# One block sum of the linear-attention branch by a DMA that adds within SBUF, and two weight splits written ahead of other steps

## The chip, the cores and the metric

The kernel runs on one core of a Trainium2 chip. The metric is the device time of one execution in microseconds. Three runs of the kernel before gave 763.68, 763.93 and 764.01 us; their median is 763.93 us.

## The reference

One layer of a decoder on 512 tokens with 16 meta tokens in front, width 1024: two branches, retention and gated linear attention (GLA), both fed by one input projection, each projected back to the width and merged by learned gates.

```
u = rms_norm(h, norm_gain)
proj = u @ w_in
(rq, rk, rv, rg, gq, gk, gv, gg, glr, m_ret, m_gla) = jnp.split(proj, points, axis=-1)
...
o_gla = gla_chunked(gq, gk, gv, log_a)
o_gla = head_rms_norm(o_gla, gla_norm_gain...).reshape(bsz, length, GLA_WIDTH)
o_gla = o_gla * jax.nn.silu(gg)

merged = sigmoid(m_ret) * (o_ret @ w_branch_ret) + sigmoid(m_gla) * (o_gla @ w_branch_gla)
return h + merged @ w_out
```

The change lies in `o_gla @ w_branch_gla`, a product of 512 x 1024 by 1024 x 1024 in float32. All else is as before.

## The kernel before, in words

**Products.** Float32 operands are split into a high part (a cast, on ScalarE, ACT in the profile) and a low part (operand minus high part, on VectorE, DVE), both in the type fp32r (line 154, `split`). Each block product is then three matmuls on TensorE (PE): high by high, high of the weights by low of the input, low of the weights by high of the input (line 318). PE is fed the whole time by such products, 24 matmuls each of 128x128 by 128x256 where a 512 x 512 block is multiplied.

**Seven products for eight.** `quad` multiplies a 2 x 2 arrangement of blocks by Winograd's scheme with seven products, numbered 1 to 7. The input's seven forms are made once: A11, A12, A22 (blocks) and S1 to S4 (sums of blocks). The weights' forms are made in each call: w11, w21 and w22 are loaded by DMAs from SP's queue, x3 and x1 are loaded the same way and then added to by a second DMA from GpSimd's queue (POOL, line 282, `accum_op`), and w11 += x3 (for product 6) and w21 += w11 (for product 4) are additions on DVE. Three PSUM tiles b, a and c take the products. `copy` moves a tile from PSUM to SBUF on ACT (line 334), `evac` adds two of them into an output block.

**GLA's branch.** `gla_branch` calls `quad` twice (j = 0 and 1, names `bg0` and `bg1` in the order of the program, both `bg` in the profile) with `early=True`: products in the order 1, 7, 6, 2, 5, 4, 3. The output blocks, `gb`, go to a buffer `kept` in DRAM by DMAs from SP's queue. The next call is the first `quad` of retention's query and key, `rqk`.

**The forms** are made in `gla_sums`, which runs beside the products, a step between two of them. There a00, a01, a10 and a11 are the blocks of GLA's output, 128 x 1024 each (tiles `og`, `og1gq`, `og`, `og1gk`). DVE turns a10 into the sum for S1 and a00 into the sum for S2. For S4 GpSimd adds a00 to a01 (line 1115), and ACT and DVE split the negative of the result (lines 1125 and 1126). The tiles of the forms' parts are `ga` (A11, A12), `ga22h` and `ga22l` (A22), `gs` (S1, S2, S4) and `gs3h`, `gs3l` (S3).

**What sets the order.** Each engine works its own queue strictly in order, and the order in a queue follows from the order of the code and from a scheduling layer that places instructions by their dependencies; a few are pinned by hand with `after`. PE's order is fixed: `pin` ties each product to the one before. Three tiles each for high and low weight parts go round (`wsplit`), so a split waits for the product three back in that ring. Six tiles `raw` hold loaded weights: SP's next load starts when DVE has read the last of an old tile. Loads and stores from SP, and the adding DMAs from POOL, share 16 DMA engines; in the profile q1 is SP's queue, q0 is POOL's.

## Time and profile before

| | |
|---|---|
| median of 3 runs | 763.93 us (763.68 to 764.01) |
| profiled execution, first to last instruction (span) | 762.2 us |
| median less span: what lies around the span | 1.7 us |
| PE busy | 750.4 us, 98% of the span |
| DVE busy | 611.2 us, 80% |
| ACT busy | 451.2 us, 59% |
| POOL busy | 133.4 us, 17% |
| mean granted TensorE clock | 0.996 of full speed |

No time is given for the profiled execution apart from its span. In the timeline's rows the first number is the start and the second the busy time in us, then engine, line, operation, out<-in, shapes; in brackets the engine's idle time ahead of the row and what ended it. Several equal rows that follow each other are one row with a count. Numbers of tiles are left out, so `bg_l<-bg_w,bg_h` is the low part of any of a call's weights, told apart by the order.

### The profile page before, as it was taken

The numbers are of one execution on the slowest core, as the hardware profiler recorded it, in microseconds if no ns is written. First come the engines' busy times: TensorE is split into PE (matmuls) and PEld (weight loads), VectorE is DVE, ScalarE is ACT, GpSimd is POOL, SyncE is SP. The second block draws the span as 40 slices with busy tenths as digits, with TensorE's granted clock in tenths as the row PEclk, the third lists the DMA queues.
The fourth block names the chain that finished last, engine by engine and source line by source line (L and its number), as shares of the span: only waits on it lengthen the run. The fifth ranks groups of instructions, "written<-read, shape, count | busy, mean of one in ns | idle before, by whom it ended". The sixth has DMA issues, their size and how long they took to land.

```text
span 762.2 us, 14057 instructions
## 1 busy us (share of the span) xinstructions
PE 750.4 (98%) x5595; PEld 701.5 (92%) x5595; DVE 611.2 (80%) x873; ACT 451.2 (59%) x764; POOL 133.4 (17%) x172
## 2 busy tenths in 40 slices
PE   9999999999989999999999999999999999999996
PEld 6799899999989999998889999889999999988996
DVE  6799877689897799778957688876787989775994
ACT  7897584666974465545646455555554756532562
POOL 2211200112231122110330100240002210111142
PEclk9999999999999999999999999999999999999999
DMA  9864321822568973753684563696477357687503
GB/s 301 277 146 106 89 84 45 185 82 70 137 168 229 295 171 91 164 144 119 176 239 125 117 161 111 166 206 154 120 166 159 93 148 193 227 196 199 136 29 111
DMA packets 99995, 116.89 MB, mean 153 GB/s; under 512 B 5717, under 2 KB 90837, under 8 KB 99673
## 3 DMA queue, kind: packets, MB, share of 16 engines
q1 hardware_dynamic: 79896, 88.19, 37.8%
q0 software_dynamic: 19744, 27.27, 19.6%
q8 instruction: 44, 0.72, 0.4%
q10 hardware_dynamic: 288, 0.53, 0.2%
q14 instruction: 23, 0.18, 0.1%
HBM read 104.44 MB, written 11.53 MB: 152 GB/s over the span
## 4 chain that ended last, share of the span: by engine, by line
PE 87%; DVE 9%; issue 2%; ACT 1%; POOL 0%; POOLq 0%; DVEq 0%
PE rv_b L318 6%; PE rg_b L318 6%; PE rqk_b L318 5%; PE rqk_c L318 4%; PE br_p L192 4%; PE br_p L193 3%; PE br_p L189 3%; PE gg_b L318 3%; PE mr_b L318 3%; PE gv_p L640 3%; PE rv_c L318 3%; PE bg_b L318 3%; PE rg_c L318 3%; PE mg_b L318 2%; PE gg_c L318 2%
## 5 line engine op out<-in xcount | busy, mean ns | idle before, releaser
L192 PE MATMUL br_p<-ol,br_h 128*128 128x512 f32 x128 | 50.6, 395 | 1.7 <-DVE ol L492 1.7
L189 PE MATMUL br_p<-oh,br_h 128*128 128x512 f32 x128 | 50.4, 394 | 0.0
L193 PE MATMUL br_p<-oh,br_l 128*128 128x512 f32 x128 | 50.3, 393 | 0.0
L154 ACT CAST rv_h<-rv_w 128x1024 fp32r<-128x1024 f32 x24 | 25.2, 1052 | 26.9 <-DVE rv_w L371 9.6
L154 DVE TENSOR_TENSOR rv_l<-rv_w,rv_h 128x1024 fp32r<-128x1024 f32 x24 | 29.3, 1221 | 9.2 <-ACT rv_h L154 9.2
L154 DVE TENSOR_TENSOR rg_l<-rg_w,rg_h 128x1024 fp32r<-128x1024 f32 x20 | 24.4, 1219 | 8.4 <-ACT rg_h L154 8.4
L192 PEld LDWEIGHTS br_p<-ol,br_h 128*128 128x128 f32 x128 | 24.0, 188 | 7.4 <-DVE ol L492 2.4
L154 ACT CAST br_h<-br_w 128x1024 fp32r<-128x1024 f32 x16 | 16.8, 1050 | 23.4 <-PE br_p L192 9.9
L282 POOL DMA_DIRECT2D rqk_x<-in_w_in_dram x8 | 10.4, 1305 | 109.5 <-DVE vl L154 66.2
L193 PEld LDWEIGHTS br_p<-oh,br_l 128*128 128x128 f32 x128 | 24.0, 188 | 5.5
L154 ACT CAST rg_h<-rg_w 128x1024 fp32r<-128x1024 f32 x20 | 21.0, 1052 | 13.2 <-PE br_p L192 5.0
L189 PEld LDWEIGHTS br_p<-oh,br_h 128*128 128x128 f32 x128 | 24.0, 188 | 5.1 <-ACT oh L491 0.2
L318 PE MATMUL rv_b<-rv_l,fh 128*128 128x256 f32 x96 | 27.1, 282 | 0.1
L318 PE MATMUL rqk_b<-fh,rqk_h 128*128 128x256 f32 (+1 forms) x96 | 27.2, 283 | 0.0
L318 PE MATMUL rqk_b<-fh,rqk_l 128*128 128x256 f32 (+1 forms) x96 | 27.1, 282 | 0.0
L318 PE MATMUL rqk_b<-fl,rqk_h 128*128 128x256 f32 (+1 forms) x96 | 27.1, 282 | 0.0
L154 DVE TENSOR_TENSOR rqk_l<-rqk_w,rqk_h 128x1024 fp32r<-128x1024 f32 x20 | 24.4, 1220 | 3.3 <-ACT rqk_h L154 3.3
L318 PE MATMUL rg_b<-rg_h,fl 128*128 128x256 f32 x96 | 27.0, 281 | 0.0
L318 PE MATMUL rv_b<-rv_h,fl 128*128 128x256 f32 x96 | 27.0, 281 | 0.0
L318 PE MATMUL rg_b<-rg_h,fh 128*128 128x256 f32 x96 | 26.9, 281 | 0.0
L318 PE MATMUL rg_b<-rg_l,fh 128*128 128x256 f32 x96 | 26.9, 281 | 0.0
L318 PE MATMUL rv_b<-rv_h,fh 128*128 128x256 f32 x96 | 26.9, 280 | 0.0
(720 smaller groups left out, 3239.4 us busy)
## 6 DMA issues: line engine op xcount, KB each, us to landing
rv_w<-in_w_in_dram SPq DMA_DIRECT2D x16, 512.0 KB, 4.2
br_w<-in_w_branch_ret_dram SPq DMA_DIRECT2D x16, 512.0 KB, 3.5
rqk_w<-in_w_in_dram SPq DMA_DIRECT2D x12, 512.0 KB, 4.5
rg_w<-in_w_in_dram SPq DMA_DIRECT2D x12, 512.0 KB, 5.4
rqk_x<-in_w_in_dram SPq DMA_DIRECT2D x8, 512.0 KB, 5.3
rqk_x<-in_w_in_dram POOLq DMA_DIRECT2D x8, 512.0 KB, 8.1
rg_x<-in_w_in_dram SPq DMA_DIRECT2D x8, 512.0 KB, 4.2
rg_x<-in_w_in_dram POOLq DMA_DIRECT2D x8, 512.0 KB, 7.7
```

The lines of the kernel that those rows point to most:

```text
L154: return nc.scalar.copy(hi, src), nc.vector.tensor_sub(lo, src, hi.bitcast(F32))
L189: m = nc.tensor.matmul(o, lh, rh, start=first, stop=False)
L192: nc.tensor.matmul(o, lh, rl, start=False, stop=False)
L193: m = nc.tensor.matmul(o, ll, rh, start=False, stop=last)
L282: x = nc.gpsimd.dma_start(t, block(0, 1), accum_op=ALU.add)
L318: m = nc.tensor.matmul(ps[t][:, :n] if wide else ps[t], l, r, start=first and j == 0, stop=kk == 3 and j == 2, skip_group_check=not fresh ...
L640: m = nc.tensor.matmul(pss[t], (al if j == 1 else ah)[t // 2, kh][:, k, c], (lo if j == 2 else hi)[:, kk, :], start=q == kk == j == 0, sto ...
```

## The change

Two edits. In `gla_sums` GpSimd's addition of a00 into a01 becomes a DMA from GpSimd's queue that adds a01 into a00, both in SBUF, 512 KB; S4's two parts are then split from a00, and `after` places them behind the last weight split written before them (`low`). In `quad`, for calls with `early`, the split of x1 for product 5 is written right behind product 2, ahead of the addition w21 += w11, of the output block `put(0, 0)` and of the copy of tile c; the addition moves behind the next step; the split of w22 for product 3 is written ahead of `put(0, 1)`. Other calls pass `ready=None` and make the splits where they did. PE's order of instructions is the same, row for row.

```diff
@@ quad, early
             product(2, A12, w21, a, True)
-            nc.vector.tensor_add(w21, w21, w11)
+            ready = prepare(5, x1)
             put(0, 0, a, x)
             x7 = copy(c, 3)
             yield
+            nc.vector.tensor_add(w21, w21, w11)
...
-        product(5, S1, x1, b, False)
+        product(5, S1, x1, b, False, ready)
...
         product(4, A22, w21, c, False)
+        ready = prepare(3, w22) if early else None
         put(0, 1, c, y)
         yield
-        product(3, S4, w22, b, False)
+        product(3, S4, w22, b, False, ready)
@@ gla_sums
-        nc.gpsimd.tensor_add(a01, a01, a00)
+        nc.gpsimd.dma_start(a00, a01, accum_op=ALU.add)
...
-        nc.scalar.mul(hi, a01, -1.0)
-        nc.vector.scalar_tensor_tensor(lo, a01, -1.0, hi.bitcast(F32), op0=ALU.mult, op1=ALU.subtract)
+        after(nc.scalar.mul(hi, a00, -1.0), low[0])
+        after(nc.vector.scalar_tensor_tensor(lo, a00, -1.0, hi.bitcast(F32), op0=ALU.mult, op1=ALU.subtract), low[1])
```

DVE's queue in the first branch call (`bg0`), from the low part for product 2 to the first split of the second call, before; `gs1`, `gs4` are the low parts of S1 and S4, `gb0` and `gb1` output blocks:

```order
L154 TENSOR_TENSOR bg0_2_l_2761<-bg0_w21_2654,bg0_2_h_2760 128x1024
L154 TENSOR_TENSOR gs1_2504<-og0_1331,gs1_2504 128x1024
L365 TENSOR_TENSOR bg0_w21_2654<-bg0_w21_2654,bg0_w11_2653 128x1024
L154 TENSOR_TENSOR bg0_5_l_2797<-bg0_x1_2656,bg0_5_h_2796 128x1024
L154 TENSOR_TENSOR ga22l0_2512<-og1gk_2521,ga22h0_2510 128x512
L154 TENSOR_TENSOR bg0_4_l_2832<-bg0_w21_2654,bg0_4_h_2831 128x1024
L1164 TENSOR_TENSOR gb0_2789<-bg0_a_2666,bg0_x1_2696 128x512
L154 TENSOR_TENSOR ga22l1_2513<-og1gk_2521,ga22h1_2511 128x512
L1126 SCALAR_TENSOR_TENSOR gs4_2503<-og1gq_2520,gs4_2503 128x1024
L1162 SCALAR_TENSOR_TENSOR gb1_2824<-bg0_b_2665,bg0_x3_2792 128x512
L154 TENSOR_TENSOR bg0_3_l_2865<-bg0_w22_2657,bg0_3_h_2864 128x1024
L154 TENSOR_TENSOR bg1_1_l_2911<-bg1_w11_2895,bg1_1_h_2910 128x1024
```

The same stretch of DVE's queue now:

```order
L154 TENSOR_TENSOR bg0_2_l_2761<-bg0_w21_2654,bg0_2_h_2760 128x1024
L154 TENSOR_TENSOR bg0_5_l_2789<-bg0_x1_2656,bg0_5_h_2788 128x1024
L154 TENSOR_TENSOR gs1_2504<-og0_1331,gs1_2504 128x1024
L369 TENSOR_TENSOR bg0_w21_2654<-bg0_w21_2654,bg0_w11_2653 128x1024
L154 TENSOR_TENSOR ga22l0_2512<-og1gk_2521,ga22h0_2510 128x512
L154 TENSOR_TENSOR ga22l1_2513<-og1gk_2521,ga22h1_2511 128x512
L1167 TENSOR_TENSOR gb0_2792<-bg0_a_2666,bg0_x1_2696 128x512
L154 TENSOR_TENSOR bg0_4_l_2832<-bg0_w21_2654,bg0_4_h_2831 128x1024
L154 TENSOR_TENSOR bg0_3_l_2860<-bg0_w22_2657,bg0_3_h_2859 128x1024
L1165 SCALAR_TENSOR_TENSOR gb1_2824<-bg0_b_2665,bg0_x3_2795 128x512
L1129 SCALAR_TENSOR_TENSOR gs4_2503<-og0_1331,gs4_2503 128x1024
L154 TENSOR_TENSOR bg1_1_l_2911<-bg1_w11_2895,bg1_1_h_2910 128x1024
```

The split for product 5 moved two places up, that for product 4 two places down, that for product 3 ahead of `gb1` and S4's, and S4's low part down to the place ahead of the second call's first split.

ACT's queue over the same stretch, before; the copies are of PSUM tiles:

```order
L154 CAST bg0_2_h_2760<-bg0_w21_2654 128x1024
L154 CAST gs1_2504<-og0_1331 128x1024
L154 CAST bg0_5_h_2796<-bg0_x1_2656 128x1024
L154 CAST ga22h0_2510<-og1gk_2521 128x512
L1125 ACTIVATE gs4_2503<-og1gq_2520 128x1024
L334 COPY bg0_x2_2758<-bg0_b_2665 128x512
L154 CAST bg0_4_h_2831<-bg0_w21_2654 128x1024
L154 CAST ga22h1_2511<-og1gk_2521 128x512
L154 CAST bg0_3_h_2864<-bg0_w22_2657 128x1024
L334 COPY bg0_x3_2792<-bg0_c_2667 128x512
```

And now:

```order
L154 CAST bg0_2_h_2760<-bg0_w21_2654 128x1024
L154 CAST bg0_5_h_2788<-bg0_x1_2656 128x1024
L154 CAST gs1_2504<-og0_1331 128x1024
L154 CAST ga22h0_2510<-og1gk_2521 128x512
L334 COPY bg0_x2_2758<-bg0_b_2665 128x512
L154 CAST ga22h1_2511<-og1gk_2521 128x512
L154 CAST bg0_4_h_2831<-bg0_w21_2654 128x1024
L154 CAST bg0_3_h_2859<-bg0_w22_2657 128x1024
L334 COPY bg0_x3_2795<-bg0_c_2667 128x512
L1128 ACTIVATE gs4_2503<-og0_1331 128x1024
```

S4's high part moved from ahead of the copy of tile b to behind the copy of tile c. In the second branch call and in all other calls the order on ACT and DVE stays. SP's queue, before:

```order
L280 DMA bg1_w21_2896<-in_w_branch_gla_dram 128x4x256
L280 DMA bg1_x1_2898<-in_w_branch_gla_dram 128x4x256
L280 DMA bg1_w22_2899<-in_w_branch_gla_dram 128x4x256
L1166 DMA kept_116<-gb0_2789 128x2x256
L1166 DMA kept_116<-gb1_2824 128x2x256
L280 DMA rqk0_w11_3139<-in_w_in_dram 128x4x256
```

and now, with the loads of the second branch call (`bg1`), stores of output blocks and the first load of `rqk`:

```order
L280 DMA bg1_w21_2896<-in_w_branch_gla_dram 128x4x256
L280 DMA bg1_x1_2898<-in_w_branch_gla_dram 128x4x256
L1169 DMA kept_116<-gb0_2792 128x2x256
L280 DMA bg1_w22_2899<-in_w_branch_gla_dram 128x4x256
L280 DMA rqk0_w11_3139<-in_w_in_dram 128x4x256
L1169 DMA kept_116<-gb1_2824 128x2x256
```

A store moved ahead of a load and the next call's first load ahead of a store. The raw tiles that the first two loads go to changed places: the load of w21 now waits for DVE's split of x1 (product 5's), that of x1 for the addition w21 += w11; before it was the other way round. On POOL the addition's place is taken by the DMA; it stands behind the adding DMA of the second call's x3 and ahead of that of its x1, waits for DVE's low part of S2, and no longer for the low part of A12, since it doesn't write to a01.

## The prediction

> **What bounds the kernel now.** I read the page's first part, then PE's waits over the whole kernel, then PE's timeline at the largest of them. The first part:

> ```profile
> PE 750.4 (98%) x5595; PEld 701.5 (92%) x5595; DVE 611.2 (80%) x873; ACT 451.2 (59%) x764; POOL 133.4 (17%) x172
> ```

> PE is busy nearly throughout: only a wait of PE, or a stretch in which its clock is lower, is there to be won. PE's waits, as instruction, releaser, and total, count and longest in us:

> ```profile
> PE br_p L192 <- DVE ol L492: 1.7, 2, 0.9
> PE bg_b L318 <- DVE bg_l L154: 1.3, 1, 1.3
> PE bg_b L318 <- ACT bg_x L334: 0.8, 1, 0.8
> ```

> The second and third lie in the branch. PE's timeline there:

> ```profile
> 222.72 0.28 PE L318 MATMUL bg_a<-ga,bg_l 128*128 128x256 f32 x1
> 223.77 0.50 PE L318 MATMUL bg_b<-gs,bg_h 128*128 128x256 f32 x2 [0.77 <-ACT bg_x L334]
> 225.56 0.38 PE L318 MATMUL bg_b<-gs,bg_l 128*128 128x256 f32 x1 [1.29 <-DVE bg_l L154]
> 229.77 0.28 PE L318 MATMUL bg_c<-ga22h,bg_h 128*128 128x256 f32 x1
> 232.60 0.40 PE L318 MATMUL bg_b<-gs,bg_h 128*128 128x256 f32 x2
> ```

> The rows are the end of product 2, the start of product 5, its first matmul with the weights' low part, and the starts of products 4 and 3, in `bg0`. PE waits first for the copy that frees tile b, then for the low part of x1: 0.77 + 1.29 = 2.06 us. The chain of waits gives what stood ahead of that low part on DVE, and how long 22 and 24 matmuls took on PE:

> ```profile
> 223.16 1.21 DVE bg_w L365
> 224.37 1.15 DVE bg_l L154
> 225.56 4.37 PE bg_b L318 x22
> ...
> 241.28 2.74 PE bg_b L318 x24
> ```

> The 22 matmuls left of product 5 took 4.37 us where 24 take 2.74 later. The half-microsecond windows say why (from:to, width, then busy time of PE, its weight loads, DVE, ACT and POOL, then granted clock, DMA share and GB/s):

> ```profile
> 226.00:226.50 0.50, 0.50 (x6) 0.50 (x5) 0.50 (x2) 0.50 (x1) 0.00 (x0) 0.82 1.06 367
> 226.50:227.00 0.50, 0.50 (x4) 0.50 (x3) 0.50 (x1) 0.42 (x1) 0.00 (x0) 0.50 1.10 377
> 229.00:229.50 0.50, 0.50 (x4) 0.50 (x4) 0.50 (x1) 0.00 (x0) 0.00 (x0) 0.50 0.79 147
> 230.00:230.50 0.50, 0.50 (x7) 0.50 (x6) 0.46 (x1) 0.50 (x1) 0.00 (x0) 1.00 0.67 195
> ```

> The granted clock falls to 0.50 shortly after the wait and is back at 1.00 by 230.0: some 3.4 us at half speed, 1.7 us of work lost. The stall so costs about twice its length. Not every wait does that; the longest elsewhere, with the clock behind it:

> ```profile
> 356.70 0.50 PE L192 MATMUL br_p<-ol,br_h 128*128 128x512 f32 x1 [0.91 <-DVE ol L492]
> ```

> ```profile
> 350.00:360.00 10.00, 9.09 (x65) 8.11 (x65) 9.97 (x16) 5.94 (x12) 0.23 (x1) 1.00 0.22 66
> ```

> 0.91 us leaves the clock at 1.00. So the threshold lies between 0.91 and 2.06 us of waiting, as far as this trace shows. [...]

> **The change part by part. First, the split for product 5.** DVE, from product 2's low part on:

> ```profile
> 218.68 1.22 DVE L154 TENSOR_TENSOR bg_l<-bg_w,bg_h 128x1024 fp32r<-128x1024 f32 x1
> 219.81 3.43 DVE L154 TENSOR_TENSOR gs<-og,gs 128x1024 fp32r<-128x1024 f32 x1
> 223.16 1.21 DVE L365 TENSOR_TENSOR bg_w<-bg_w,bg_w 128x1024 f32<-128x1024 f32 x1
> 224.30 1.21 DVE L154 TENSOR_TENSOR bg_l<-bg_x,bg_h 128x1024 fp32r<-128x1024 f32 x1
> 225.43 0.68 DVE L154 TENSOR_TENSOR ga22l<-og1gk,ga22h 128x512 fp32r<-128x512 f32 x1
> 226.03 1.22 DVE L154 TENSOR_TENSOR bg_l<-bg_w,bg_h 128x1024 fp32r<-128x1024 f32 x1
> ```

> S1's low part took 3.43 us against 1.22 of the same operation one row up, while GpSimd's addition, which the change removes, ran beside it:

> ```profile
> 217.12 1.33 POOL L282 DMA_DIRECT2D bg_x<-in_w_branch_gla_dram  x1 [1.46 <-DMA bg_x<-in_w_branch_gla_dram]
> 218.85 3.31 POOL L1115 TENSOR_TENSOR og1gq<-og1gq,og 128x1024 f32<-128x1024 f32 x1 [0.39 <-DVE ga L154]
> ```

> Now x1's low part stands directly behind product 2's: DVE starts it at 219.82 (ACT's high part, in its new place, ends near 219.4) and ends near 221.0; S1's low part follows, 221.0 to 222.2 at 1.22 a piece. Both are there before product 2 ends at 222.72 + 0.12 (the pitch, 2.74 / 24). ACT's copy of tile b, which waited behind S4's high part, has only half a cast ahead of it and ends near 221.4. So product 5 runs from 222.84 without a wait for 2.74 us, to 225.58, where before product 4 began at 229.77: **4.19 us** won: 2.06 of waiting, 1.7 of clock, the rest short gaps.

> **The addition w21 += w11, `gb0` and the other split.** They move behind, and product 4 needs its low part of w21. From S1's end at 222.2, by the starts' distance of 1.14 (223.16 to 224.30) and 0.60 for the half-width (225.43 to 226.03): the addition to 223.3, two halves of A22 to 224.5, `gb0` to 225.1, product 4's low part to 226.26. The third matmul, 0.23 us in, needs it: a wait of 0.45 us, half of the 0.91 that left the clock alone. Product 4 ends at 225.58 + 0.45 + 2.74 = 228.8. If I have ACT or DVE 0.5 us wrong here, the wait is 0 to 0.95. The split for product 3 then ends at 227.4 and isn't late.

> **S4 by a DMA.** GpSimd's 3.31 us of addition go. In their place stands an issue behind the one at 217.12, so at about 218.45, 512 KB. No DMA within SBUF that adds is in the trace; the nearest are adding DMAs from DRAM (KB, us from issue to landing):

> ```profile
> bg_x<-in_w_branch_gla_dram POOLq DMA_DIRECT2D x1, 512.0 KB, 7.2
> ...
> kr<-kept POOLq DMA_DIRECT2D x1, 512.0 KB, 5.5
> ...
> rqk_x<-in_w_in_dram POOLq DMA_DIRECT2D x1, 512.0 KB, 10.6
> ```

> The first is the one issued at 217.12: it landed at 224.3. The second is a single one of the same row length as S4's, in an empty queue; the third the slowest of all. By them S4's sum lands between 218.45 + 5.5 = 224.0 and 218.45 + 10.6 = 229.05. I take the time behind the one in front: 224.3 plus 512 KB at the queue's rate while that one moved,

> ```profile
> q0 software_dynamic: 191, 0.20, 124.6%
> ```

> 0.20 MB in one us (packets, MB, share of the engines): 2.6 us, so **227.0**, the queue working in order. [...]

> Is there room on the DMA engines? Windows at the place:

> ```profile
> 217.00:219.00 2.00, 1.98 (x18) 1.77 (x17) 1.80 (x3) 2.00 (x3) 1.48 (x2) 1.00 0.00 0
> ...
> 222.50:225.50 3.00, 1.00 (x7) 0.60 (x5) 3.00 (x4) 2.31 (x4) 0.00 (x0) 1.00 0.04 6
> ```

> Their share is 0.04 between 222.5 and 225.5, so 3 us are idle there. The loads of the second call come earlier as well, since DVE frees the raw tiles earlier, and take part of that.

> Then ACT's high and DVE's low part of S4, rows of this operation:

> ```profile
> 222.19 1.06 ACT L1125 ACTIVATE gs<-og1gq 128x1024 fp32r<-128x1024 f32 x1 [1.32 <-POOL og1gq L1115]
> 228.37 1.21 DVE L1126 SCALAR_TENSOR_TENSOR gs<-og1gq,gs 128x1024 fp32r<-128x1024 f32 x1
> ```

> 227.0 + 1.06 + 1.21 = 229.27; PE's second matmul needs the low part, 0.12 after the start, so product 3 begins at 229.15 (landing + 2.15), 0.3 us behind 228.85. Before it began at 232.60: **3.45 us** left. Queued behind S4's two waiting instructions are the first and later splits of the second call, on ACT and DVE both; before, its first split stood directly behind too, so only the shift of the landing counts.

> **What is late next.** From 232.60 to 340 PE has no wait of over 0.2 us before. The tightest place that doesn't move with PE is product 2 of the first `rqk` call:

> ```profile
> 253.08 1.23 DVE L371 TENSOR_TENSOR rqk_w<-rqk_w,rqk_x 128x1024 f32<-128x1024 f32 x1 [1.35 <-DMA rqk_x<-in_w_in_dram]
> 254.83 1.21 DVE L154 TENSOR_TENSOR rqk_l<-rqk_w,rqk_h 128x1024 fp32r<-128x1024 f32 x1
> ```

> ```profile
> 257.94 2.92 PE rqk_c L318 x24
> ```

> The low part is ready at 256.04, PE needs it at 257.94 + 0.23: 2.1 us of slack. It hangs on an adding DMA, which hangs on loads that are issued when raw tiles come free, in part with PE. If nothing of that moves, 2.1 us of the gain are left; if it moves by 1 us, 3.1. I take 3.1: **0.35 us** off.

> **The sum.** 4.19 won, 0.45 for product 4's wait, 0.3 for product 3's, 0.35 for `rqk`: 3.1 us. The profiled execution's span was 762.2, with 1.7 us around it at the median of 763.93; so 759.1 and 760.8 at the median. Ends: no wait for anything new gives 4.19 (759.7); the `rqk` bound 2.1 (761.8).

> **Rivals.** *S4's sum is late, but not very* (0.18). It lands at 228.3, 1.3 us after my value, as when the second call's loads share the engines. With the sum landed by 226.7 product 3 could begin right behind product 4, at 228.85, which is 232.60 - 228.85 = 3.75 us earlier than before; each us of landing after that takes one. So the gain is 3.75 - (228.3 - 226.7) = 2.15, with `rqk` hardly late any more: 761.8. At the upper row, 229.05, PE waits 2.35 us, over the 2.06 that went with the low clock: 1.7 more are lost, and it is 764.2. For it: two adding DMAs in one queue. Against: 3 us of idle engines.

> *The low clock isn't from this wait* (0.06). Two gaps of 0.77 and 1.29 us with two matmuls between them need not lower it; something else does then, and the stretch at 0.50 stays. The gain is 3.1 - 1.7 = 1.4: 762.5. [...] For it: neither gap is much longer than the 0.91 that did nothing. Against: the clock is 1.00 everywhere near but right behind them.

> *Slower: PE waits for S4's DMA instead* (0.10). The adding DMA reads and writes SBUF, and a plain load in this trace took this long under load:

> ```profile
> wo_w<-in_w_out_dram SPq DMA_DIRECT2D x1, 512.0 KB, 13.7
> ```

> 218.45 + 13.7 = 232.15: product 3 begins at 234.3, 1.7 us later than before, after 5.4 us of waiting, so at half clock, 1.7 more: +3.4, 767.3. ACT and DVE stand with it. It decides from a landing at 228.8 on, where the wait passes 2.06 us and the gain is gone; at 230.3 it is slower by 1.5. For it: the operation isn't in the trace. Against: the `kr` row's 5.5.

> *Other causes* (0.04): no change.

> **The numbers.** Forecast 0.62. A measurement of this kernel can tell about 0.2%, 1.5 us. Faster by more: the forecast and 0.08 of the late one, 0.70. Within: 0.08 of the late one, the clock's 0.06 and 0.04, 0.18. Slower: 0.10 and 0.02, 0.12. The range: 759.5, the full 4.19 with 0.2 for the runs' spread, up to 763.4, which takes in both the late sum and the clock's case and leaves out the slower rival and the late one's upper end.

> **What would show it.** Right: product 5 of `bg0` without a wait, starting at about 222.8, no clock under 1.00 there, S1's low part at 1.2 us, a wait of under 0.6 us ahead of product 4 and of product 3, S4's sum landed near 227, `rqk`'s product 2 about 3 us earlier. Wrong: a landing after 228.8, or PE waiting over 1 us for `gs`; a clock of 0.50 with no wait before it; or a wait of over 0.5 us in `rqk`, by which the gain is given back.

## The result, and the profile after

| | before | after |
|---|---|---|
| median of 7 runs, us | 764.01 (763.68 to 764.66) | 761.37 (760.62 to 762.36) |
| profiled execution, span, us | 762.2 | 759.1 |
| PE busy, us | 750.4 | 749.1 |

The ratio is 0.9968, with a 95% interval from 0.9958 to 0.9977: 2.6 us faster, against 3.1 forecast (761.37 against 760.8, in the range of 759.5 to 763.4). The span is the 759.1 that the sum gave; the median lies 2.3 us above that span, where before it lay 1.7 above, since the profiled execution, at 760.91 us, is one of the faster of the seven.

PE's waits of the whole kernel, as before by instruction, releaser, total, count and longest:

```profile
PE br_p L192 <- DVE ol L495: 1.7, 2, 0.9
PE warm_p L577 <- DVE warm L574: 1.2, 1, 1.2
PE gf L913 <- ACT gon L1002: 0.5, 1, 0.5
PE bg_b L318 <- DVE gs L1129: 0.3, 1, 0.3
```

The two waits for x1's low part and for the copy of tile b (1.3 and 0.8) are gone; a new one of 0.3, for S4's low part, has come. PE's timeline at the ends of product 2, at the first matmuls of products 5 and 4, and at the first two of product 3:

```profile
223.04 0.28 PE L318 MATMUL bg_a<-ga,bg_l 128*128 128x256 f32 x1
223.16 0.40 PE L318 MATMUL bg_b<-gs,bg_h 128*128 128x256 f32 x2
...
226.06 0.39 PE L318 MATMUL bg_c<-ga22h,bg_h 128*128 128x256 f32 x1
...
229.12 0.28 PE L318 MATMUL bg_b<-gs,bg_h 128*128 128x256 f32 x1
229.67 0.39 PE L318 MATMUL bg_b<-gs,bg_h 128*128 128x256 f32 x1 [0.27 <-DVE gs L1129]
```

Product 5 follows product 2 after the usual 0.12 us. From product 2's last matmul to product 4's first it is 3.02 us (223.04 to 226.06), where it was 7.05 (222.72 to 229.77). The windows have the clock at 1.00 throughout:

```profile
222.50:230.50 8.00, 7.73 (x63) 7.34 (x63) 7.72 (x9) 5.44 (x6) 0.00 (x0) 1.00 1.06 299
230.50:262.00 31.50, 31.50 (x271) 31.50 (x270) 22.92 (x25) 15.32 (x20) 5.51 (x5) 1.00 1.02 276
```

DVE's timeline shows both edits: x1's low part stands in front, and S1's takes 1.22 us instead of 3.43.

```profile
218.81 1.22 DVE L154 TENSOR_TENSOR bg_l<-bg_w,bg_h 128x1024 fp32r<-128x1024 f32 x1
219.94 1.22 DVE L154 TENSOR_TENSOR bg_l<-bg_x,bg_h 128x1024 fp32r<-128x1024 f32 x1
221.08 1.22 DVE L154 TENSOR_TENSOR gs<-og,gs 128x1024 fp32r<-128x1024 f32 x1
```

And the chain of waits shows where S4 stands now (start, length, what):

```profile
218.02 9.09 DMA og<-og1gq
...
227.29 1.07 ACT gs L1128
...
228.39 1.24 DVE gs L1129
...
229.67 5.75 PE bg_b L318 x47
```

The DMA was issued at 218.02 and landed at 227.11. From there it is the two parts of the split and PE, with nothing between.

Traces start the branch at times that differ by up to 1.4 us between kernels that are the same up to there: product 2's last matmul starts at 222.72 us before, at 223.04 and 223.69 in two traces of the changed kernel, and at 224.08 in the kernel with GpSimd's addition and the new order. Part of it is there at the kernel's start: the fifth `gv_p` matmul starts at 5.97 before and at 6.12 in the changed kernel's first trace. So I compare a stretch: from the last matmul of product 2 in `bg0` to the first of `rqk`, in the trace before:

```profile
222.72 0.28 PE L318 MATMUL bg_a<-ga,bg_l 128*128 128x256 f32 x1
...
254.85 0.28 PE L318 MATMUL rqk_b<-xh,rqk_h 128*128 128x264 f32 x1
```

That is 32.13 us. After the change the second of these rows is

```profile
251.81 0.28 PE L318 MATMUL rqk_b<-xh,rqk_h 128*128 128x264 f32 x1
```

so 251.81 - 223.04 = 28.77 us: 3.36 us were won in the stretch. The span is shorter by 3.1 only (762.2 - 759.1), since the branch started 0.32 us later in this execution. Below this stretch is called the branch stretch.

### The profile page after: what moved, and what is told of

The parts are those of the page before. It is cut to its first block, busy times and chain, and to the rows that moved or that the text cites. A ratio compares the mean times of both kernels' runs of the same rounds, so it can differ in the third digit from the quotient of the medians.

```text
span 759.1 us, 14062 instructions
## 1 busy us (share of the span) xinstructions
PE 749.1 (99%) x5595; PEld 700.2 (92%) x5595; DVE 609.4 (80%) x873; ACT 450.7 (59%) x764; POOL 130.8 (17%) x172
## 4 chain that ended last, share of the span: by engine, by line
PE 82%; DVE 10%; issue 3%; DMA 2%; ACT 1%; POOL 1%; POOLq 0%; DVEq 0%; ACTq 0%
PE rv_b L318 6%; PE rg_b L318 6%; PE rqk_b L318 4%; PE br_p L192 4%; PE br_p L193 3%; PE rqk_c L318 3%; PE br_p L189 3%; PE gg_b L318 3%; PE gv_p L643 3%; PE rv_c L318 3%; PE rg_c L318 3%; PE mg_b L318 2%; PE mr_b L318 2%; PE bg_b L318 2%; PE gg_c L318 2%
## 5 line engine op out<-in xcount | busy, mean ns | idle before, releaser
L192 PE MATMUL br_p<-ol,br_h 128*128 128x512 f32 x128 | 50.6, 395 | 1.7 <-DVE ol L495 1.7
L154 ACT CAST rv_h<-rv_w 128x1024 fp32r<-128x1024 f32 x24 | 25.3, 1052 | 27.0 <-DVE rv_w L372 9.6
L154 DVE TENSOR_TENSOR rv_l<-rv_w,rv_h 128x1024 fp32r<-128x1024 f32 x24 | 29.4, 1223 | 9.2 <-ACT rv_h L154 9.2
L154 DVE TENSOR_TENSOR rg_l<-rg_w,rg_h 128x1024 fp32r<-128x1024 f32 x20 | 24.4, 1222 | 8.3 <-ACT rg_h L154 8.3
L192 PEld LDWEIGHTS br_p<-ol,br_h 128*128 128x128 f32 x128 | 24.0, 188 | 7.4 <-DVE ol L495 2.4
L154 ACT CAST br_h<-br_w 128x1024 fp32r<-128x1024 f32 x16 | 16.8, 1050 | 23.1 <-PE br_p L192 9.9
L154 ACT CAST rg_h<-rg_w 128x1024 fp32r<-128x1024 f32 x20 | 21.0, 1051 | 13.2 <-PE br_p L192 5.0
L282 POOL DMA_DIRECT2D rqk_x<-in_w_in_dram x8 | 10.4, 1306 | 105.4 <-PE rv_b L318 47.9
L154 DVE TENSOR_TENSOR rqk_l<-rqk_w,rqk_h 128x1024 fp32r<-128x1024 f32 x20 | 24.4, 1221 | 4.0 <-ACT rqk_h L154 4.0
L318 PE MATMUL rv_b<-rv_l,fh 128*128 128x256 f32 x96 | 27.0, 282 | 0.2 <-DVE rv_l L154 0.2
L318 PE MATMUL rqk_b<-fh,rqk_h 128*128 128x256 f32 (+1 forms) x96 | 27.2, 283 | 0.0
L318 PE MATMUL rqk_b<-fh,rqk_l 128*128 128x256 f32 (+1 forms) x96 | 27.1, 282 | 0.0
L318 PE MATMUL rqk_b<-fl,rqk_h 128*128 128x256 f32 (+1 forms) x96 | 27.1, 282 | 0.0
L318 PE MATMUL rg_b<-rg_h,fl 128*128 128x256 f32 x96 | 27.0, 281 | 0.0
L318 PE MATMUL rv_b<-rv_h,fl 128*128 128x256 f32 x96 | 27.0, 281 | 0.0
L318 PE MATMUL rg_b<-rg_h,fh 128*128 128x256 f32 x96 | 26.9, 281 | 0.0
L318 PE MATMUL rg_b<-rg_l,fh 128*128 128x256 f32 x96 | 26.9, 281 | 0.0
L318 PE MATMUL rv_b<-rv_h,fh 128*128 128x256 f32 x96 | 26.9, 280 | 0.0
## 6 DMA issues: line engine op xcount, KB each, us to landing
rv_w<-in_w_in_dram SPq DMA_DIRECT2D x16, 512.0 KB, 4.1
br_w<-in_w_branch_ret_dram SPq DMA_DIRECT2D x16, 512.0 KB, 3.5
rqk_w<-in_w_in_dram SPq DMA_DIRECT2D x12, 512.0 KB, 5.0
rg_w<-in_w_in_dram SPq DMA_DIRECT2D x12, 512.0 KB, 5.3
rqk_x<-in_w_in_dram SPq DMA_DIRECT2D x8, 512.0 KB, 3.9
rqk_x<-in_w_in_dram POOLq DMA_DIRECT2D x8, 512.0 KB, 7.7
rg_x<-in_w_in_dram SPq DMA_DIRECT2D x8, 512.0 KB, 3.5
rg_x<-in_w_in_dram POOLq DMA_DIRECT2D x8, 512.0 KB, 6.7
```

Of the source, the lines that this page charges most:

```text
L154: return nc.scalar.copy(hi, src), nc.vector.tensor_sub(lo, src, hi.bitcast(F32))
L192: nc.tensor.matmul(o, lh, rl, start=False, stop=False)
L282: x = nc.gpsimd.dma_start(t, block(0, 1), accum_op=ALU.add)
L318: m = nc.tensor.matmul(ps[t][:, :n] if wide else ps[t], l, r, start=first and j == 0, stop=kk == 3 and j == 2, skip_group_check=not fresh ...
```

## The experiments

Theory: the wait ahead of product 5, with the half clock behind it, is what the change takes away; it needs the order and the DMA together, since GpSimd's addition holds DVE up whatever runs there; and S4's landing then decides. Rivals: one of the edits does it alone; the clock falls for another cause; S4's landing has slack.

**Only the splits moved.** GpSimd's addition and S4's old place stay:

```diff
-        nc.gpsimd.dma_start(a00, a01, accum_op=ALU.add)
+        nc.gpsimd.tensor_add(a01, a01, a00)
...
-        after(nc.scalar.mul(hi, a00, -1.0), low[0])
-        after(nc.vector.scalar_tensor_tensor(lo, a00, -1.0, ...), low[1])
+        nc.scalar.mul(hi, a01, -1.0)
+        nc.vector.scalar_tensor_tensor(lo, a01, -1.0, ...)
```

> Only the splits are moved; GpSimd's addition and S4's split stay as before. Theory: GpSimd's addition (3.3 us) now holds up the low part of x1 instead of S1's (about 3.4 us instead of 1.2), S1's low part ends near 224.4, and S4's high part on ACT still stands ahead of the copy of tile b. Product 5 of bg0 waits about 1.6 us instead of 2.06, product 4 then waits some 2.4 us for its low part, which stands behind S4's. Nearly nothing is won: 763 to 766 us. Rival, by which the moved split carries the change and the DMA is a detail: product 5 waits for nothing, 761 us.

Measured: 765.55 us, ratio 1.0022 (1.0013 to 1.0031), 1.7 us slower than before. PE's timeline has four waits:

```profile
224.04 0.38 PE L318 MATMUL bg_b<-gs,bg_h 128*128 128x256 f32 x1 [0.76 <-ACT bg_x L334]
224.70 0.38 PE L318 MATMUL bg_b<-gs,bg_h 128*128 128x256 f32 x1 [0.28 <-DVE gs L154]
228.79 0.39 PE L318 MATMUL bg_c<-ga22h,bg_h 128*128 128x256 f32 x1 [1.20 <-ACT bg_x L334]
229.91 0.38 PE L318 MATMUL bg_c<-ga22h,bg_l 128*128 128x256 f32 x1 [0.61 <-DVE bg_l L154]
```

1.04 us at product 5 and 1.81 at product 4, where 1.6 and 2.4 were expected. On DVE the operation that now stands beside GpSimd's addition is the long one, and S1's is short again:

```profile
220.08 3.43 DVE L154 TENSOR_TENSOR bg_l<-bg_x,bg_h 128x1024 fp32r<-128x1024 f32 x1
223.43 1.21 DVE L154 TENSOR_TENSOR gs<-og,gs 128x1024 fp32r<-128x1024 f32 x1
```

```profile
219.12 3.30 POOL L1118 TENSOR_TENSOR og1gq<-og1gq,og 128x1024 f32<-128x1024 f32 x1 [0.22 <-DVE ga L154]
```

So it isn't S1's operation that is slow but the one that runs there, as the theory had it. The windows show a stretch at 0.50 that begins behind product 4's waits, not behind product 5's:

```profile
230.00:230.50 0.50, 0.50 (x5) 0.50 (x6) 0.50 (x2) 0.00 (x0) 0.30 (x1) 0.98 0.00 0
230.50:233.50 3.00, 3.00 (x17) 3.00 (x16) 2.22 (x2) 0.00 (x0) 1.01 (x1) 0.50 0.78 230
233.50:234.00 0.50, 0.50 (x4) 0.50 (x4) 0.00 (x0) 0.00 (x0) 0.00 (x0) 0.60 1.30 256
```

From the means, 0.02 us of its start lie in the first row and 0.4 us of its end in the last, beside the 3.0: 3.4 us, as before the change, at another place. It went with the wait. That the moved split carries the change alone is refuted.

**The changed kernel with GpSimd's addition for the DMA.** The ties that place S4's split late stay:

```diff
-        nc.gpsimd.dma_start(a00, a01, accum_op=ALU.add)
+        nc.gpsimd.tensor_add(a01, a01, a00)
...
-        after(nc.scalar.mul(hi, a00, -1.0), low[0])
-        after(nc.vector.scalar_tensor_tensor(lo, a00, -1.0, ...), low[1])
+        after(nc.scalar.mul(hi, a01, -1.0), low[0])
+        after(nc.vector.scalar_tensor_tensor(lo, a01, -1.0, ...), low[1])
```

> As the changed kernel, S4's split in its new late place too, but the sum by GpSimd's addition instead of the DMA. Theory: the copy of tile b isn't late any more, but GpSimd still holds up DVE by about 2.2 us, so S1's low part ends near 224.4 and product 5 waits 1.4 us for it, product 4 up to 1.2 us; product 3 starts near 231.3, 1.3 us earlier than before: 762.3 to 763.2 us. So the DMA is worth 1.5 to 2 us beside the order. If the order alone carries it: 761 us. If a wait of 1.4 us lowers the clock, product 5 has a stretch at 0.50; if the clock follows something else, it is at 1.00 or the stretch lies elsewhere.

Measured: 763.03 us, ratio 0.9991 (0.9983 to 1.0000); the branch stretch takes 30.72 us, 1.4 less than before, though the medians differ by 0.8 only (763.84 against 763.03); the profiled execution, at 763.98 us, is the slowest of the eleven. PE waits twice:

```profile
225.61 0.39 PE L318 MATMUL bg_b<-gs,bg_h 128*128 128x256 f32 x1 [1.13 <-DVE gs L154]
229.32 0.39 PE L318 MATMUL bg_c<-ga22h,bg_h 128*128 128x256 f32 x1 [0.81 <-ACT bg_x L334]
```

```profile
224.00:230.00 6.00, 4.05 (x32) 3.58 (x31) 6.00 (x8) 3.22 (x4) 0.00 (x0) 1.00 0.65 199
```

The clock stays at 1.00 over both, which together are nearly as long as the 2.06 us before the change, but with 2.9 us between them. The DMA's worth beside the order is 763.03 - 761.37 = 1.7 us, as expected: what GpSimd's addition costs by holding up DVE, where x1's low part takes 3.44 us beside it instead of 1.22.

**Only the DMA.** The weights' splits as before, S4 by the DMA and tied late. Against the changed kernel:

```diff
-            ready = prepare(5, x1)
+            nc.vector.tensor_add(w21, w21, w11)
...
-            nc.vector.tensor_add(w21, w21, w11)
...
-        product(5, S1, x1, b, False, ready)
+        product(5, S1, x1, b, False)
...
-        ready = prepare(3, w22) if early else None
...
-        product(3, S4, w22, b, False, ready)
+        product(3, S4, w22, b, False)
```

> Only the DMA, with S4's split behind the last weight split before it; the weights' splits in their old places. Theory: product 5 waits only some 0.3 us, for S1's low part takes 1.2 us and x1's ends at 223.3; but on ACT S4's high part, which waits for the DMA until 227, now stands ahead of the second half of A22, and product 4 stops in its middle for 2.5 us or more, with a stretch at half clock behind it. Nothing won: 763 to 764.5 us. If the clock doesn't follow the wait: 762.4 to 763.4. Rival, by which the DMA alone carries the change: 761 us.

Measured: 765.56 us, ratio 1.0026 (1.0015 to 1.0037): slower than before. Product 5 waits for nothing, but product 4 waits 4.6 us, and the whole of it, not its second half:

```profile
230.70 0.58 PE L318 MATMUL bg_c<-ga22h,bg_h 128*128 128x256 f32 x1 [4.58 <-ACT bg_x L334]
```

```profile
227.65 1.06 ACT L1125 ACTIVATE gs<-og 128x1024 fp32r<-128x1024 f32 x1 [4.45 <-DMA og<-og1gq]
228.62 0.60 ACT L154 CAST ga22h<-og1gk 128x512 fp32r<-128x512 f32 x1
229.12 1.04 ACT L154 CAST bg_h<-bg_w 128x1024 fp32r<-128x1024 f32 x1
230.07 0.57 ACT L334 COPY bg_x<-bg_c 128x512 f32<-128x512 f32 x1
```

I had seen A22's second half behind the waiting instruction on ACT and overlooked the copy that frees tile c, which stands behind as well. The size was missed; that nothing is won by the DMA alone, and why, came out. The profiled execution, at 767.35 us, is the second slowest of the seven. Its stretch at half clock is 6.8 us long, which alone takes 3.4 / 765.5 = 0.0044 off its mean granted clock (0.993); four of the seven have 0.997 or 0.999, so no such stretch.

**Without the two ties.** The changed kernel, S4's split where the scheduler puts it:

```diff
-        after(nc.scalar.mul(hi, a00, -1.0), low[0])
-        after(nc.vector.scalar_tensor_tensor(lo, a00, -1.0, ...), low[1])
+        nc.scalar.mul(hi, a00, -1.0)
+        nc.vector.scalar_tensor_tensor(lo, a00, -1.0, ...)
```

> The changed kernel without the two ties that hold S4's split behind the split of w22. Theory: on ACT S4's high part stands ahead of the copy of tile b and waits for the DMA until 227, so product 5 starts near 228.6, after 5.8 us of waiting; at half clock behind it product 3 starts some 3.2 us later than before: 767 us. If the clock doesn't follow the wait: 765.5 us. Rival, by which the place of S4's split is a detail: 761 us.

Measured: 768.22 us, ratio 1.0059 (1.0046 to 1.0071), 6.9 us slower than the changed kernel. Product 5 waits as expected (5.4 us for the copy of tile b):

```profile
228.63 0.79 PE L318 MATMUL bg_b<-gs,bg_h 128*128 128x256 f32 x2 [5.39 <-ACT bg_x L334]
```

```profile
227.00:227.50 0.50, 0.00 (x0) 0.00 (x0) 0.00 (x0) 0.45 (x1) 0.00 (x0) 0.62 1.10 385
227.50:233.50 6.00, 4.87 (x23) 4.87 (x24) 3.56 (x4) 3.98 (x6) 1.30 (x1) 0.50 0.54 137
233.50:234.00 0.50, 0.50 (x4) 0.50 (x4) 0.00 (x0) 0.01 (x1) 0.00 (x0) 0.55 1.16 186
```

The stretch at half clock is 6.8 us long here, twice what I reckoned with, and PE is idle for 1.5 us of it: (6.8 - 1.5) / 2 = 2.65 us of work are lost where 1.7 were reckoned. By this estimate it is most of the 1.2 us by which the time is above the expectation.

**S4's sum on DVE.** No DMA and no GpSimd; the scheduler puts the addition directly behind product 2's low part:

```diff
-        nc.gpsimd.dma_start(a00, a01, accum_op=ALU.add)
+        nc.vector.tensor_add(a01, a01, a00)
```

S4's split reads a01, tied as in the change.

> The changed kernel with S4's sum as an addition on DVE instead of the DMA; the scheduler puts it directly behind product 2's low part. Theory: nothing holds DVE up, it only has 1.14 us more in front of the rest, so product 5 waits 0.4 us and product 4 about 1.0 us; product 3 waits for no DMA any more. Some 0.8 us more than the changed kernel: 762.2 us, clock at 1.00. Rival, by which the DMA itself is what is needed: 763.9 us as before.

Measured: 762.12 us, ratio 0.9976 (0.9967 to 0.9986), branch stretch 29.53. The kernel with GpSimd's addition and the same order took 763.03 and 30.72. So the DMA isn't needed as such: most of what it brings is that GpSimd doesn't work beside DVE: x1's and S1's low parts take 1.22 us each in this kernel. The DMA's branch stretch is shorter by 29.53 - 28.77 = 0.76 us, less than the 1.14 that the addition puts in front of the rest on DVE, and the intervals of the two ratios overlap. It shows as a wait at product 4, shorter than the 1.0 expected:

```profile
227.76 0.38 PE L318 MATMUL bg_c<-ga22h,bg_l 128*128 128x256 f32 x1 [0.55 <-DVE bg_l L154]
```

**S4's landing put off.** The changed kernel with DMAs of S2's low part to unused DRAM buffers ahead of S4's in POOL's queue; here with one of 512 KB:

```diff
+    spare = dp.tile([P, 4, 256], F32R, name="spare")
...
-        nc.gpsimd.dma_start(a00, a01, accum_op=ALU.add)
+        x = nc.gpsimd.dma_start(spare[:, :4], gforms[S2][1][:, :4])
+        after(nc.gpsimd.dma_start(a00, a01, accum_op=ALU.add), x)
```

With 256 KB:

> The changed kernel with a 256 KB DMA to an unused DRAM buffer ahead of S4's DMA in POOL's queue; all else in the same order. At 0.20 MB a us S4's sum lands some 1.3 us later, near 228.4, and product 3 of bg0 waits about 1.6 us instead of 0.3. Theory, by which a short wait costs its length and the clock falls only from some amount over 1.1 and up to 1.8 us: 1.3 us more than the changed kernel, 762.7 us, if 1.6 us is below that amount, 764.4 if above; the clock rows say which. Rival, by which what lies between S4 and product 3 has slack: no difference, 761.4.

With 512 KB:

> The same with 512 KB: S4's sum lands near 229.7, product 3 waits about 2.9 us, over what lowered the clock before. Theory: 2.6 us more of waiting and 1.7 of clock, 765.7 us, slower than before the change. If the clock doesn't follow the wait: 764 us and no row under 1.00.

Measured: 761.58 us with 256 KB (0.9974, 0.9964 to 0.9983) and 762.30 with 512 (0.9981, 0.9972 to 0.9990). I had sized these DMAs wrong: against the changed kernel's first trace they put the landing off by 0.4 and 0.9 us, not 1.3 and 2.6. The plain write to DRAM moved faster than the 0.20 MB a us of the adding DMA: the 512 KB landed near 225.2 (issued at 218.27, 6.9 us to landing), some 1.2 us behind x3's DMA in front of it (217.46 + 6.5), so by this estimate 0.4 MB a us. So they don't decide between the cases, but they give the slope. PE's waits for S4 are

```profile
230.07 0.38 PE L318 MATMUL bg_b<-gs,bg_h 128*128 128x256 f32 x1 [0.68 <-DVE gs L1131]
```

```profile
230.60 0.38 PE L318 MATMUL bg_b<-gs,bg_h 128*128 128x256 f32 x1 [0.87 <-DVE gs L1131]
```

with the clock at 1.00 in the branch for both. With 1024 and 1536 KB (two and three such DMAs in a row):

> As the kernels with 256 and 512 KB ahead of S4's DMA, now 1024 KB. The 512 KB put the landing off by 0.9 us; the second 512 KB meet the loads and should take more, some 1.2 us. S4's sum lands near 229.2, product 3 waits about 2.1 us in one piece. Theory, by which the amount of waiting lowers the clock, from some 1.8 us on: 2.1 + 1.7 us more than the changed kernel less 0.3, 764.9 us, a stretch at 0.50 behind the wait. If one piece of 2 us does not lower it: 763.2 us.

> The same with 1536 KB: the landing near 230.5, product 3 waits about 3.4 us. Theory: 3.1 us more of waiting and 1.7 of clock, 766.2 us, 2.3 us slower than before the change, as the slower rival of the prediction had it. If such a wait does not lower the clock: 764.5 us.

Measured: 765.11 us with 1024 KB (1.0016, 1.0002 to 1.0029; single runs from 763.0 to 767.7) and 767.44 with 1536 (1.0045, 1.0032 to 1.0059), where 764.9 and 766.2 were expected. S4's DMA landed 10.4 and 11.1 us after its issue. PE waits in two pieces, since the first matmul of product 3 runs as soon as the high part is there; with 1024 KB:

```profile
231.89 0.38 PE L318 MATMUL bg_b<-gs,bg_h 128*128 128x256 f32 x1 [1.80 <-ACT gs L1133]
233.15 0.58 PE L318 MATMUL bg_b<-gs,bg_h 128*128 128x256 f32 x1 [0.88 <-DVE gs L1134]
```

```profile
232.00:232.50 0.50, 0.27 (x1) 0.07 (x1) 0.50 (x1) 0.50 (x1) 0.00 (x0) 0.69 1.09 381
232.50:239.00 6.50, 5.85 (x27) 5.85 (x28) 4.60 (x5) 1.94 (x3) 1.31 (x1) 0.50 1.13 309
```

With 1536 KB the waits are 3.20 and 0.88. The clock fell in both traces, for 6.8 us with 1024 KB and for 3.4 with 1536. It did not in every execution with 1024 KB: five of the twelve, from 762.99 to 764.05 us, have a mean granted clock of 0.999, the seven others, from 765.07 to 767.66, of 0.993 to 0.997. One stretch of 3.4 us at half clock takes 1.7 / 762 = 0.0022 off the mean, so the five had none in the branch; the profiled one, at 767.13 and 0.993, is among the slowest. So the slower rival of the prediction is a real mechanism, only at a landing that this change doesn't have.

**The changed kernel again, and S4's DMA ahead of x3's.** The second ties the adding DMA of the second call's x3 behind S4's, in `quad`:

```diff
-        nc.gpsimd.dma_start(a00, a01, accum_op=ALU.add)
+        parts["s4"] = nc.gpsimd.dma_start(a00, a01, accum_op=ALU.add)
...
                     x = nc.gpsimd.dma_start(t, block(0, 1), accum_op=ALU.add)
+                    if t is x3 and name == "bg1":
+                        after(x, parts["s4"])
```

> The changed kernel with S4's DMA ahead of the adding DMA of the second call's x3 in POOL's queue. Theory: it lands some 2.6 us earlier, near 224, and product 3 waits for nothing: 0.3 to 0.4 us less, 761.0 us, within the spread of the runs; x3 lands 2.6 us later, near 227, still ahead of the addition that reads it at 231. Rival: x3 then is late, product 6 of bg1 waits, and it is slower than the changed kernel.

> The changed kernel once more, on the same chip as the next three. If the first measurement stands: 761.4 us, 2.6 us faster than before the change, no row of the clock under 1.00 in the branch, product 3 of bg0 waiting 0.3 us.

> S4's DMA ahead of x3's, once more beside the changed kernel: 0.3 to 0.9 us less than it (0.3 by the wait that its trace shows gone, 0.9 by the first medians).

Measured: the order with S4 first 760.45 (0.9957, 0.9944 to 0.9969) and, beside the changed kernel on one chip, 760.55 (0.9954, 0.9941 to 0.9967); the changed kernel there 761.34 (0.9964, 0.9951 to 0.9977). On that chip the five runs of the one lie from 760.39 to 761.16, of the other from 760.90 to 761.85. S4's DMA and x3's in the trace, as issues with their landing:

```profile
og<-og1gq POOLq DMA_DIRECT2D x1, 512.0 KB, 6.1
bg_x<-in_w_branch_gla_dram POOLq DMA_DIRECT2D x1, 512.0 KB, 9.2
```

S4's is issued at 217.63 and lands at 223.7; x3's lands near 227.4, ahead of its reader at 230.74. PE waits for nothing in the branch, which takes 28.38 us. The median is lower by 0.8 us. The branch stretch is shorter by 0.39 against the changed kernel's first trace (28.77 - 28.38), but by 0.04 only between the two traces taken beside each other (28.43 - 28.39), and the intervals of the two ratios overlap. So the traces show a gain of 0 to 0.4 us, by how early S4 lands in the execution, and the rest stays open.

All kernels in which S4's landing is moved, ordered by it (time from product 2's last matmul to the landing, then the branch stretch):

| kernel | landing, us | wait for S4, us | branch stretch, us |
|---|---|---|---|
| S4 first | 0.8 | none | 28.38 |
| S4 first, again | 1.2 | none | 28.39 |
| changed, again | 3.7 | none listed | 28.43 |
| changed | 4.1 | 0.27 | 28.77 |
| 256 KB ahead | 4.5 | 0.68 | 29.19 |
| 512 KB ahead | 5.0 | 0.87 | 29.67 |
| 1024 KB ahead | 6.7 | 1.80 + 0.88 | 34.07 |
| 1536 KB ahead | 8.3 | 3.20 + 0.88 | 34.55 |
| before (sum by GpSimd) | | | 32.13 |

Up to 3.7 us the landing costs next to nothing, then each us costs about one, and in the profiled executions at 6.7 and 8.3 the clock comes on top. As an estimate: without its 1.7 us of clock the row of 1536 KB would be at 32.9, so without the clock the break-even with before, as it stands, would lie between 7 and 8 us. Each row is one execution: the two of the changed kernel land 0.4 us apart, the two with S4 first as well.

## Why the prediction was right

**Product 5.** Forecast 4.19 us, from no wait and no low clock. The wait is gone and the clock is at 1.00. From product 2's last matmul to product 4's first it takes 3.02 us (223.04 to 226.06) where it took 7.05: 4.03 were won. The missing 0.16 lie in product 5 itself, 2.90 us (223.16 to 226.06) where 2.74 were reckoned.

**Product 4.** Forecast a wait of 0.45. None is listed, but product 4's first four matmuls start at 226.06, 226.28, 226.43 and 226.65, up to 0.22 us apart instead of 0.12; the low part of w21 was ready at 225.16 + 1.22 = 226.38, just ahead of the third, which needs it. From product 4's first matmul to product 3's it takes 3.06 us where it took 2.83 (229.77 to 232.60): 0.23 are lost. So the mechanism is there, at half of the forecast size.

**S4.** The forecast landing was 227.0, by the queue working in order at 0.20 MB a us: 2.6 us behind x3's DMA. It landed at 227.11, 2.8 us behind x3's (224.31), in a trace in which the branch runs 0.3 us later. Product 3's second matmul started 0.55 us behind its first instead of 0.12, so 0.43 are lost, of which the view lists 0.27 as idle; 0.3 were forecast. The table bears out the formula: it has the landing free up to 3.7 us behind product 2's last matmul, the prediction up to 226.7 - 222.72 = 4.0, and about one us for each behind that.

**`rqk`.** The one term that came out at nothing: 0.35 us were taken off for its adding DMA. PE waits for nothing there. The addition that hung on it began at 253.08; now

```profile
248.94 1.23 DVE L372 TENSOR_TENSOR rqk_w<-rqk_w,rqk_x 128x1024 f32<-128x1024 f32 x1 [0.25 <-DMA rqk_x<-in_w_in_dram]
```

it is 4.1 us earlier, while PE is 3.0 earlier. The adding DMA was issued at 243.99 and is now at 241.07, 2.9 us earlier, much as PE; I had put that at 1 us. And it took 7.8 us to land instead of 9.0; why isn't shown.

**The sum.** 4.03 won, 0.23 lost at product 4 and 0.43 at product 3: 3.4 us, the 3.36 of the stretch, against 3.1 forecast. The four terms were off by 0.16, 0.22, 0.13 and 0.35, two in each direction, and in part cancel. That the span came to the forecast number is chance, by the 0.32 us later at the start of the stretch; the medians moved by 2.6.

**The clock.** The rival that it falls for another cause has the traces against it. Of the fourteen, six have a stretch at 0.50 in the branch, each right behind 1.8 us or more of PE's waiting within 3.4 us; in the eight others, whose waits are shorter or further apart, the clock stays at 1.00 there. What the runs correct is the price. In the prediction's words, "the stall so costs about twice its length": that holds for the profiled execution, but in the traces the loss comes in pieces of 3.4 us at half clock: none in eight of them, one in three, two in three.

For the median the price is open. The kernel before was timed 63 more times beside the experiments. In 27 of these executions the mean granted clock was 0.999 or 1.000, which leaves no room for a stretch of 3.4 us; their median is 763.69 us, that of the other 36 is 763.97. So the 1.7 us that the prediction read off the profiled execution don't show as a difference between executions. The traces give a possible reason: the branch of the kernel with GpSimd's addition and the new order, which has no stretch, starts 1.36 us later than the one before (224.08 against 222.72). If the executions without a stretch are those that reach the branch late, they lose ahead of it much of what they save in it; there are no traces of them, so this isn't shown. That the profiled execution had the stretch was in part chance, and so it is in part luck that the forecast from it came near the medians.

Two details of the prediction: among PE's waits before stands one of 1.2 us, `warm_p`, ahead of the kernel's first matmul. The 0.91 is the longest of the others; that it leaves the clock at 1.00 stands. And product 4's end, by its own sum 225.58 + 0.45 + 2.74 = 228.77, is taken further as 228.85, which makes the wait for S4 0.08 us shorter.

**The late and the slow rival.** Their mechanism is there, at a later landing. The slower one put the crossing at a landing of 228.8, that is 6.1 us behind product 2's last matmul; the runs have it between 5.0 (1.7 us faster than before) and 6.7 (1.2 slower).

## What to carry to other kernels

Where PE is the bound, a wait can cost its length again in lowered clock, so two waits far apart can be cheaper than the same time close together (2.06 us of waiting within 2.6 us cost 1.7 more here, 1.13 and 0.81 us with 2.9 between them left the clock at 1.00): look at the granted clock for some 8 us behind each, since with 1024 KB it was back at 1.00 only 7.1 us behind the first wait (231.89 to 239.0), and at more than one execution. Work moved off one engine pays by what stood beside it: GpSimd's addition cost 2.2 us on DVE (3.43 and 3.44 against 1.22) with either of the two operations that it met. And an instruction that waits for a DMA belongs in its queue behind everything that PE needs first: that one place was worth 6.9 us here, more than the whole change.

## What the runs showed of the hardware

| kernel | idle in the 3.4 us ahead | idle in the first 3.4 us at 0.50 | length at 0.50 |
|---|---|---|---|
| before | 2.06 | 0.00 | 3.4 |
| splits only | 1.81 | 0.00 | 3.4 |
| 1536 KB ahead | 3.03 | 0.44 | 3.4 |
| 1024 KB ahead | 1.80 | 0.88 | 6.8 |
| only the DMA | 3.14 | 1.44 | 6.8 |
| no ties | 3.41 | 1.51 | 6.8 |
| the eight others, most in any 3.4 us | 1.13 | | none |

- If the clock is set by such windows in every execution, the same wait can fall into one of them or be divided between two, and where they lie differs, as the record's start does (4.455 and 4.949 us). The single runs with 1024 KB, spread over 4.7 us and with mean clocks from 0.993 to 0.999, fit that. It wasn't shown, since the profiles hold one execution each.
- A DMA that adds 512 KB within SBUF took 6.1 and 6.5 us at the head of its queue (S4 first, two traces) and 9.1 and 8.5 right behind x3's of 512 KB (the changed kernel, two traces), much as one that adds from DRAM: x3's took 6.0 to 7.2 at the head and 9.2 behind S4's.
- In the changed kernel's two traces S4's adding DMA landed 2.8 and 2.6 us behind x3's, and with S4 first x3's landed 3.7 and 3.3 behind S4's; the plain 512 KB write to DRAM landed 1.2 us behind x3's.
